# Fewer products in the FFN's down projection, set between the up products, on one core

## The chip, the cores and the metric

The kernel runs on one core of one Trainium2 chip. Its time is the device time of one execution in microseconds (us); of several runs the median counts. The engines of the core are named as in the profile: PE multiplies matrices, PEld is its weight load, DVE is the vector engine, ACT the scalar engine, POOL the GpSimd engine, SP the engine that issues most of the transfers. Each engine works off its own queue in the order in which the program wrote it.

## The reference, cut to what matters

The reference is one layer of a backbone over 1024 latent tokens of width 1024 with 256 context tokens: a state-space mixer (S5) with a gated linear unit, then a SwiGLU feed-forward network (FFN) with 2816 hidden units, and a last RMS norm. The change is in the FFN alone:

```python
h_l = modulate(rms_norm(x, norm_ffn[i]), m_l[3][:, None], m_l[4][:, None])
x = x + m_l[5][:, None] * swiglu(h_l, ffn_w1[i], ffn_w3[i], ffn_w2[i])
...
return rms_norm(x, norm_final)
```

Here `swiglu(h, w1, w3, w2)` is `(silu(h @ w1) * (h @ w3)) @ w2`. The two products with w1 and w3 are the up projection, the one with w2 the down projection. `m_l[5]` is a factor for each output column.

## The kernel before, in words

**Numbers.** All products are to float32 accuracy. An operand x is split into a high part, `hi`, which is x cast to the type fp32r, and a low part, `lo`, which is x minus `hi`. A product is then three matmuls: high by high, high by low, low by high. ACT makes the high part (a copy that casts, in `t_split` at line 1201, `split` at 1002, `gate_up` at 1270). The low part is a subtraction through the helper `tt`, so it stands at line 70 in the profile; for weights POOL does it (the argument `E`), for gated activations DVE.

**Tiling.** The 2816 hidden units are 22 tiles of 128, `ft` = 0 to 21. The 1024 tokens are held as 8 groups `s` of 128 and as two halves `n` of 512. `Y` holds the running sum x in SBUF and takes the results of the down projection. The up projection of tiles 0 and 1 is plain (`up_plain`). From tile 2 (`NPL`) on, `up` uses seven products instead of eight for the two token halves and the two halves of the inner dimension (a Strassen scheme in Winograd's form): product j of tile ft, called U0 to U6 below, is twelve matmuls, four blocks of 128 by three (`mm4`, `mm3`, lines 1259 to 1261), each 128x128 by 128x512. Its weight operand is a combination of four blocks `raw[:, 0..3]` of w1 and w3, which POOL forms in place (`prep`), and which is split into one of four slots of `ring`. A slot is free again when the product that used it is done.

**After an up product** DVE adds its PSUM bank to running sums in `t0` to `t3`, ACT applies SiLU, and `gate_up` multiplies and splits the gated result into the regions that the down projection reads as weights.

**Down projection.** After each `up(ft)`, `down([ft])` runs 16 chains of three matmuls, one for each token group s and each half of the output columns, over four PSUM buffers `pd`; DVE adds each chain to `Y` (128x512). The last `down([20, 21], True)` takes two tiles in one and also does the last norm. The w2 tile arrives in `w2raw` by a transfer on SP's queue (`raw2`); `load2` multiplies it on DVE with the column factor and splits it (1024 wide, POOL the low part).

**What sets the order.** The order of each queue is the order of the calls in the code, written out by hand (`manual_schedule`); the framework adds the waits. While `down([ft])` runs on PE, `prep(ft + 1)` steps between its chains prepare the next weights on POOL. The next tile's U0 is issued ahead of `down([ft])`. Transfers `raw13` fetch the blocks of w1 and w3 in three pieces as `raw` comes free.

Of the kernel before, what the change touches and what calls it, by code (L numbers as in the profile page):

```python
# [10 lines left out]
F32 = mybir.dt.float32  # L11
# [6 lines left out]
P = 128  # L18
# [19 lines left out]
def s5_ffn_kernel(tc, a, out):  # L38
# [3 lines left out]
    with ctx:  # L42
        ctx.enter_context(tc.manual_schedule())
        sb = ctx.enter_context(tc.tile_pool(name="sb", bufs=1))
        def region(tag, kb, dt=F32):
            return sb.tile([P, int(kb * 256)], dt, tag=tag, name=tag)

        def view(reg, kb, shape, parts=P):
            off = int(round(kb * 256))
            n = int(np.prod(shape))  # L50
            v = reg[:parts, off:off + n]
            if len(shape) > 1:
                names = "abcdef"[:len(shape)]
# [15 lines left out]
        def tt(o, x, y, op, eng=V):  # L69
            eng.tensor_tensor(out=o, in0=x, in1=y, op=op)  # L70
# [1175 lines left out]
        def gb(ft):  # L1246
            return GB[ft == NFT - 1]

        def raw2(ft):
            SY.dma_start(w2raw, a["w2"][ft * P:(ft + 1) * P])  # L1250

        def load2(ft):
            tt(w2raw, w2raw, MB[:, 1], MUL)
            split(w2raw, gb(ft)[2:], E)
            if ft + 1 < NFT:
                raw2(ft + 1)

# [102 lines left out]
        def prep(ft):  # L1360

            if ft > NPL:
                op_split(ft, 1, raw[:, 1])
                yield
# [11 lines left out]
        def mm(ft, j):  # L1376
            pu = pu_()
            mm4(pu, OP_[ft, j], BV[j], True, True)
            return pu

        def up(ft, pu, at={}):

            t0, t1, t2, t3 = tmp
            more = ft + 1 < NFT

            def go(j):
                if j in at:
                    at[j]()

            S.copy(t0, pu)  # L1390
            op_split(ft, 4, raw[:, 3])
            go(0)
            if more:
                raw13(ft + 1, 0, 1)
                raw13(ft + 1, 2, 4)
            tt(t1, mm(ft, 1), t0, ADD)
            S.activation(t1, t1, AF.Silu)
            op_split(ft, 5, raw[:, 1])
            if more:
                raw13(ft + 1, 1, 2)  # L1400
            go(1)
            tt(t0, mm(ft, 2), t0, ADD)
            op_split(ft, 6, s5)
            go(2)
            tt(t2, mm(ft, 3), t0, ADD)
            go(3)
            if more:
                op_split(ft + 1, 0, raw[:, 0])
            pu = mm(ft, 4)
            nx = prep(ft + 1) if ft == NFT - 2 else iter(())  # L1410
            next(nx, None)
            next(nx, None)
            tt(t3, t2, pu, SUB)
            tt(t1, t1, t3, MUL)
            gate_up(ft, 0, t1)
            tt(t0, mm(ft, 5), t0, ADD)
            next(nx, None)
            pu = mm(ft, 6)
            tt(t0, pu, t0, ADD)
            S.activation(t0, t0, AF.Silu)  # L1420
            tt(t2, pu, t2, ADD)
            pu = mm(ft + 1, 0) if more else None
            tt(t0, t0, t2, MUL)
            gate_up(ft, 1, t0)
            for _ in nx:
                pass
            return pu

        def down(fts, last, *others):
            for s in range(T):  # L1430
                for n in range(2):
                    pd = pf([512])
                    x2 = Y[:, 4 * n:4 * n + 4, s]
# [44 lines left out]
        h2s(7, tba[1], 1)  # L1478
        raw2(0)
        rest = iter(())  # L1480
        up_plain(0, 0, rest, {2: lambda: together(h2t_steps(7, pf, tba[1], 0), h2t_steps(7, pf, tba[1], 1)), 3: lambda: mod_row(1, pf)})
# [13 lines left out]
        pF = psF.__enter__()  # L1495
        NPU[0] = 4
        pu = mm(NPL, 0)
        down([NPL - 1], False, prep(NPL))

# [3 lines left out]

        for ft in range(NPL, NFT - 1):
            load2(ft)
            pu = up(ft, pu, {j: t1_go for j in range(4)} if ft == NPL else {})
            if ft < NFT - 2:
                down([ft], False, prep(ft + 1))
        up(NFT - 1, pu, {2: lambda: load2(NFT - 1)})
        SY.dma_start(NFb.rearrange("p k n -> p (k n)"), a["norm_final"].to_broadcast([P, D]))  # L1510
# [60 lines left out]
```

## Time and profile before

| | |
|---|---|
| timed runs | 1083.35, 1086.05, 1090.47 us; median 1086.05 us |
| profiled execution | span 1084.0 us from the first to the last instruction; no other time of it is listed |
| matmuls | 6088 |
| PE, DVE, POOL, ACT busy | 990.4, 762.3, 631.4, 418.7 us |
| the stretch with up products of seven | about 496 to 1054 us |

In the profile's groups a name such as `ru` or `c` is a memory region (buffer numbers left out), `pu` and `pd` are the PSUM banks of up and down products; `out<-in` names what is written and read, followed by partitions x elements and type. A count stands behind x. Times are us, means of one instruction ns. In the timeline a row gives start, duration, engine, line and operation; in square brackets the idle time before it and who ended it. A row of the windows view gives, for a stretch of the span, the busy time of each engine with its count of instructions, then the granted PE clock, the share of the transfer engines, and GB/s.

### The profile page before, as it was taken

How to read it: one execution, taken by the hardware profiler on the slowest of the kernel's cores; microseconds unless marked ns; L12 is line 12 of the kernel's file. 1: busy time of each engine (PE TensorE's matmuls, PEld its weight loads, DVE VectorE, ACT ScalarE, POOL GpSimd, SP SyncE). 2: the span in 40 equal slices, each digit the busy share in tenths (PEclk: the TensorE clock that was granted, in tenths of full speed). 3: DMA queues.
4: the chain of work that ended last, by engine and by line, in shares of the span. 5: the costliest groups of instructions: out<-in, count | busy, mean ns of one | idle time of the engine just before them, and what ended most of it. 6: DMA issues, size and time to landing. Idle time of an engine off the chain costs nothing.

```text
span 1084.0 us, 16631 instructions
## 1 busy us (share of the span) xinstructions
PE 990.4 (91%) x6088; PEld 790.4 (73%) x6088; DVE 762.3 (70%) x1783; ACT 418.7 (39%) x833; POOL 631.4 (58%) x501
## 2 busy tenths in 40 slices
PE   4898795656899999999999999999999999999997
PEld 1466521345799997887888888888888888888875
DVE  8979699970665686898766666666766666666657
ACT  4477620453964565423122222222222222222236
POOL 4599666881274364966565555665555555556563
PEclk9998997987999999999999999999999999999999
DMA  8966679675333102110111111111011111111104
GB/s 310 318 124 125 187 231 312 185 142 118 104 114 116 42 2 78 59 38 21 58 59 59 59 59 59 59 59 32 31 56 59 59 59 59 60 59 59 55 23 156
DMA packets 54946, 104.60 MB, mean 96 GB/s; under 512 B 4432, under 2 KB 25168, under 8 KB 53840
## 3 DMA queue, kind: packets, MB, share of 16 engines
q1 hardware_dynamic: 46656, 85.57, 23.7%
q0 software_dynamic: 3888, 14.16, 7.0%
q10 hardware_dynamic: 4320, 3.81, 1.1%
q8 instruction: 48, 0.79, 0.3%
q14 instruction: 34, 0.28, 0.1%
HBM read 83.20 MB, written 6.16 MB: 82 GB/s over the span
## 4 chain that ended last, share of the span: by engine, by line
PE 71%; DMA 9%; POOL 6%; DVE 6%; ACT 5%; issue 2%; SPq 1%; ACTq 0%; DVEq 0%; POOLq 0%
PE pu L1261 11%; PE pu L1260 11%; PE pu L1259 11%; PE pd L1259 7%; PE pd L1260 7%; PE pd L1261 7%; PE pe L1024 3%; PE pe L1025 3%; PE pe L1023 3%; DVE ru L70 2%; POOL c L70 2%; DMA c<-in_ada_w 2%; DMA kd<-r 1%; PE pm L514 1%; DVE rxa L70 1%
## 5 line engine op out<-in xcount | busy, mean ns | idle before, releaser
L70 POOL TENSOR_TENSOR c<-rxc,c 128x512 fp32r<-128x512 f32 x128 | 167.8, 1326 | 185.1 <-ACT c L1201 180.2
L70 DVE TENSOR_TENSOR ru<-pd,ru 128x512 f32<-128x512 f32 x336 | 226.5, 690 | 0.0
L1259 PE MATMUL pu<-ra,c 128*128 128x512 f32 x432 | 168.4, 390 | 0.6 <-ACT ra L1201 0.3
L1261 PE MATMUL pu<-ra,c 128*128 128x512 f32 x432 | 168.4, 390 | 0.6 <-POOL c L70 0.6
L1260 PE MATMUL pu<-ra,c 128*128 128x512 f32 x432 | 168.2, 389 | 0.6 <-DVE ra L70 0.6
L1201 ACT CAST c<-rxc 128x512 fp32r<-128x512 f32 x128 | 76.8, 617 | 188.0 <-POOL rxc L70 107.3
L1259 PE MATMUL pd<-c 128*128 128x512 f32 x336 | 131.0, 390 | 0.7 <-DVE ru L70 0.7
L1260 PE MATMUL pd<-c 128*128 128x512 f32 x336 | 130.7, 389 | 0.0
L1261 PE MATMUL pd<-c 128*128 128x512 f32 x336 | 130.7, 389 | 0.0
L70 DVE TENSOR_TENSOR ru<-pu,ru 128x512 f32<-128x512 f32 x84 | 57.8, 688 | 83.2 <-PE pu L1261 52.4
L70 POOL TENSOR_TENSOR c<-ru,c 128x1024 fp32r<-128x1024 f32 x22 | 53.0, 2407 | 81.7 <-ACT c L1002 73.0
L1261 PEld LDWEIGHTS pu<-ra,c 128*128 128x128 f32 x432 | 81.1, 188 | 18.5 <-POOL c L70 1.7
L1259 PEld LDWEIGHTS pu<-ra,c 128*128 128x128 f32 x432 | 81.1, 188 | 18.1 <-ACT ra L1201 0.8
L1260 PEld LDWEIGHTS pu<-ra,c 128*128 128x128 f32 x432 | 81.1, 188 | 17.7 <-POOL c L70 0.9
L1259 PE MATMUL pu<-c,c 128*128 128x512 f32 x192 | 74.9, 390 | 0.0
L1261 PE MATMUL pu<-c,c 128*128 128x512 f32 x192 | 74.7, 389 | 0.0
L1260 PE MATMUL pu<-c,c 128*128 128x512 f32 x192 | 74.7, 389 | 0.0
L1259 PEld LDWEIGHTS pd<-c 128*128 128x128 f32 x336 | 63.1, 188 | 15.0 <-DVE ru L70 1.9
L1261 PEld LDWEIGHTS pd<-c 128*128 128x128 f32 x336 | 63.1, 188 | 13.2
L1260 PEld LDWEIGHTS pd<-c 128*128 128x128 f32 x336 | 63.1, 188 | 12.9
L70 POOL TENSOR_TENSOR c<-rxc,rxa 128x1024 f32<-128x1024 f32 x30 | 62.0, 2138 | 16.2 <-PE pw L655 10.4
L70 DVE TENSOR_TENSOR ru<-ru,rxa 128x512 f32<-128x512 f32 (+1 forms) x62 | 62.5, 1008 | 7.1 <-ACT ru L1420 3.1
(333 smaller groups left out, 2137.3 us busy)
## 6 DMA issues: line engine op xcount, KB each, us to landing
c<-in_ada_w SPq DMA_DIRECT2D x64, 256.0 KB, 5.4
ru<-in_w SPq DMA_DIRECT2D x22, 512.0 KB, 3.6
c<-c POOLq DMA_DIRECT2D x20, 512.0 KB, 6.7
rxc<-in_w SPq DMA_DIRECT2D x38, 256.0 KB, 4.5
rxc<-in_w SPq DMA_DIRECT2D x19, 512.0 KB, 5.1
ra<-in_ada_w SPq DMA_DIRECT2D x10, 512.0 KB, 11.9
ru<-in_xT SPq DMA_DIRECT2D x4, 1024.0 KB, 8.5
ra<-kd SPq DMA_DIRECT2D x16, 256.0 KB
```

Source lines behind the costliest of these rows:

```text
L70: eng.tensor_tensor(out=o, in0=x, in1=y, op=op)
L514: PE.matmul(pm[32 * b:32 * b + 2], sc3[:, k, 1 - h:3 - h], ada_tile(i), start=i < 4, stop=i >= 60, tile_position=(0, 32 * b))
L1023: PE.matmul(pz, h_[:, k], wH[:, k], start=n == 0, stop=False)
L1024: PE.matmul(pz, h_[:, k], wL[:, k], start=False, stop=False)
L1025: PE.matmul(pz, l_[:, k], wH[:, k], start=False, stop=n == 7)
L1201: S.copy(o[0], x)
L1259: PE.matmul(pu, wh, bh, start=start, stop=False)
L1260: PE.matmul(pu, wh, bl, start=False, stop=False)
L1261: PE.matmul(pu, wl, bh, start=False, stop=stop)
```

## The change

Tiles 2 to 19 are now taken in nine pairs (f, f+1), f = 2, 4, ..., 18 (`PAIRS`). The down projection of a pair is a product of two by two blocks (token halves by hidden tiles, hidden tiles by column halves), and it too is done by seven products, D1 to D7, with twelve matmuls each: four token groups by three. Tiles 20 and 21 keep the plain `down`, as does tile 1.

- **Order.** One list `seq` fixes the order on PE. For each f after the first: U0 U1 D6 D2 D5 D3 U2 D4 U3 U4 U5 U6 of tile f, where the D are those of the pair before, then for tile f+1 U0 D1 U1 U2 D7 U3 U4 U5 U6, where the D are of the pair itself. (The text marks products of tile f+1 with a dash: U0' to U6'.)
- **Weights' ring.** D products take their w2 operand from the same four-slot ring: `produce(i + 4)`, called after product i, makes the operand of product i+4. For D1 and D6, D4 it also forms block combinations of w2 on POOL, 512 wide.
- **w2.** There are two raw tiles (`w2r`, the second in a new region `RW` of 6 KB); DVE multiplies each with the column factor (`gate2`, after U3 and U4 of tile f).
- **Gated activations.** `post_u` writes the four blocks to `rA`, `rB`, `rC`, `t3` and combines them with DVE (`after_u` too); ACT makes the high parts and DVE the low parts in `GS`, at places spread over `post_u`, `after_u` and `post_d`.
- **PSUM.** D1, D7, D6, D5, D4 run in two tiles of two banks (`XT`), D2 and D3 in the four banks `UT` that the U products rotate through. D7, D6, D5 and D3 add onto what stands in the banks. After each D, `d_adds` adds the banks to quarters of `Y`: two adds of 128x1024 from `XT`, or four of 128x512 from `UT`.
- **Y.** `to_diff` and `from_diff` turn parts of `Y` to differences and back once (four adds of 1024 each on DVE, after U5 of tile 2 and after U3 and U5 of tile 20).
- The reserve for descriptors of POOL's transfers is set to 8192 bytes.

```diff
+        RW = region("rw", 6)
...
-        w2raw = view(RU, 32, [D])
+        w2r = [view(RU, 32, [D]), view(RW, 0, [D])]
...
+        def gate2(ft):
+            tt(w2r[ft % 2], w2r[ft % 2], MB[:, 1], MUL)
...
-        def up(ft, pu, at={}):
...
+        XT = [pF.tile([P, 2, 512], F32, tag=f"x{i}", name=f"xt{i}") for i in range(2)]
+        UT = [pF.tile([P, 512], F32, tag=f"u{i}", name=f"ut{i}") for i in range(4)]
...
+        rA, rB, rC = R0[:, 0:512], R0[:, 1036:1548], view(RW, 4, [512])
...
+        PAIRS = range(NPL, NFT - 2, 2)
+        seq = []
+        for f in list(PAIRS) + [NFT - 2]:
+            U = [("U", f, j) for j in range(7)]
+            if f == NPL:
+                seq += U
+            else:
+                M = {j: ("D", f - 2, j) for j in range(2, 7)}
+                seq += [U[0], U[1], M[6], M[2], M[5], M[3], U[2], M[4]] + U[3:]
+            if f in PAIRS:
+                U = [("U", f + 1, j) for j in range(7)]
+                seq += [U[0], ("D", f, 1), U[1], U[2], ("D", f, 7)] + U[3:]
+        seq += [("U", NFT - 1, j) for j in range(7)]
...
+        def cut(o, x):
+
+            t_split(o, x, V)
+
+        def produce(i):
...
+            if kind == "D":
+                x = w2_op(j)
+                (b11, b12), (b21, b22) = WB
+                if j == 6:
+                    tt(b12, b22, b11, SUB, E)
+                elif j == 4:
+                    tt(b21, b21, b12, SUB, E)
+                t_split(o, x, E)
+                if j == 1:
+                    tt(b11, b12, b11, SUB, E)
+                    tt(b12, b22, b12, SUB, E)
+                if j == 4:
+                    raw2(ft + 2)
+                    raw2(ft + 3)
+                return
+            x = (raw[:, 0], raw[:, 1], raw[:, 0], raw[:, 2], raw[:, 3], raw[:, 1], s5)[j]
+            t_split(o, x, E)
+            if j == 0:
+                tt(s5, raw[:, 2], raw[:, 3], ADD, E)
+            elif j == 1:
+                tt(raw[:, 2], raw[:, 0], raw[:, 2], SUB, E)
+                tt(raw[:, 0], s5, raw[:, 0], SUB, E)
+            elif j == 3:
+                tt(raw[:, 1], raw[:, 1], raw[:, 0], SUB, E)
+                if ft + 1 < NFT:
+                    raw13(ft + 1, 0, 1)
...
+        def d_mm(i):
...
+            for s, pd in d_banks(i, j):
+                cs_ = slice(s * P, s * P + P)
+                for n, (w, b) in enumerate(((gh, wh), (gh, wl), (gl, wh))):
+                    PE.matmul(pd, w[:, cs_], b, start=j in (1, 2, 4) and n == 0, stop=n == 2,
+                              skip_group_check=j not in (1, 2, 4))
+
+        def d_adds(i, j):
...
+            if j in (2, 3):
+                for s, pd in d_banks(i, j):
+                    y = Y[:, k0:k0 + 4, s0 + s]
+                    tt(y, y, pd.rearrange("p (k n) -> p k n", k=4), op)
+            else:
+                for h in range(2):
+                    y = quad(k0, s0, h)
+                    tt(y, y, XT[h].rearrange("p s (k n) -> p s k n", k=4), op)
...
+        def post_u(i, ft, j):
+
+            pu, plain, f = u_bank(i), ft >= NFT - 2, ft % 2 == 0
+            if j == 0:
+                S.copy(t0, pu)
+            elif j == 1:
+                tt(t1, pu, t0, ADD)
+                S.activation(t1, t1, AF.Silu)
...
+            elif j == 4:
+                tt(t3, t2, pu, SUB)
...
+                    r = rA if f else rC
+                    tt(r, t1, t3, MUL)
+                    cut(GS[0], r)
...
+            else:
+                tt(t0, pu, t0, ADD)
+                S.activation(t0, t0, AF.Silu)
+                tt(t2, pu, t2, ADD)
...
+                elif f:
+                    tt(rB, t0, t2, MUL)
+                    tt(rA, rA, rB, SUB)
+                else:
+                    tt(t3, t0, t2, MUL)
+                    tt(rA, t3, rA, SUB)
+
+        def after_u(ft, j):
...
+            if j == 0:
+                hi(GS[1], rA)
+                tt(rC, rA, rC, SUB)
+                lo(GS[1], rA)
+                hi(GS[2], rC)
+            elif j == 1:
+                tt(rB, rB, t3, ADD)
+                hi(GS[3], rB)
+                lo(GS[2], rC)
+
+        def post_d(i, j):
+
+            if j == 1:
+                hi(GS[1], rA)
+            d_adds(i, j)
+            if j == 1:
+                lo(GS[1], rA)
+            elif j == 6:
+                lo(GS[3], rB)
+            elif j == 2:
+                hi(GS[0], t3)
+                lo(GS[0], t3)
...
+        for i, (kind, ft, j) in enumerate(seq):
+            if i:
+                (u_mm if kind == "U" else d_mm)(i)
+            if kind == "D":
+                post_d(i, j)
+            else:
+                post_u(i, ft, j)
+                after_u(ft, j)
+                if ft in PAIRS and j in (3, 4):
+                    gate2(ft + j - 3)
+            produce(i + 4)
+            if kind == "U":
+                if ft == NPL and j < 4:
+                    t1_go()
+                if ft == NPL and j == 5:
+                    to_diff()
...
+    nc = bacc.Bacc("TRN2", target_bir_lowering=False, num_devices=1, dynamic_dma_scratch_size=8192)
```

The functions `hi` and `lo` are one ACT copy that casts and one DVE subtraction.

More of the change, by code (lines that the diff above doesn't have):

```diff
@@ L1373, in prep, with pd_ @@
             tt(raw[:, 1], raw[:, 1], raw[:, 0], SUB, E)
+            raw13(ft + 1, 0, 1)
             yield
[L1376 to L1379, printed above, removed]
-        def up(ft, pu, at={}):
[L1383 to L1427, printed above, removed]
+        def pd_(i):
+            return ([XT[0][:, 0], XT[1][:, 0]] + UT[1:])[i % 5] if XT is not None else pf([512])
+        XT = None
         def down(fts, last, *others):
@@ new lines, in quad, with to_diff, from_diff, hi @@
+        def quad(k0, s0, h):
+            return Y[:, k0:k0 + 4, s0 + 2 * h:s0 + 2 * h + 2].rearrange("p k s n -> p s k n")
+        def to_diff():
+            for h in range(2):
+                tt(quad(4, 0, h), quad(4, 0, h), quad(4, 4, h), SUB)
+                tt(quad(4, 0, h), quad(4, 0, h), quad(0, 0, h), SUB)
+        def from_diff(h):
+            tt(quad(4, 0, h), quad(4, 0, h), quad(4, 4, h), ADD)
+            tt(quad(4, 0, h), quad(4, 0, h), quad(0, 0, h), ADD)
+        def hi(o, x):
+            S.copy(o[0], x)
@@ new lines, in after_u @@
+        def after_u(ft, j):
+            if not (ft > NPL and ft <= NFT - 2 and ft % 2 == 0):
+                return
+            if j == 0:
[15 more added lines that the diff above has]
+                lo(GS[3], rB)
+            elif j == 2:
+                hi(GS[0], t3)
+                lo(GS[0], t3)
@@ L1502, in t1_go @@
                 next(rest, None)
[L1504 to L1509, printed above, removed]
+        u_mm(0)
+        down([NPL - 1], False, prep(NPL))
+        raw2(NPL)
+        raw2(NPL + 1)
+        for i, (kind, ft, j) in enumerate(seq):
[3 more added lines that the diff above has]
+                post_d(i, j)
+            else:
+                post_u(i, ft, j)
[8 more added lines that the diff above has]
+                    to_diff()
+                if ft == NFT - 2 and j in (3, 5):
+                    from_diff(j // 4)
+                if ft == NFT - 2 and j == 4:
+                    load2(NFT - 2)
+                if ft == NFT - 1 and j == 2:
+                    load2(NFT - 1)
         SY.dma_start(NFb.rearrange("p k n -> p (k n)"), a["norm_final"].to_broadcast([P, D]))
```

62 lines of the change are left out of this document (49 added, 13 removed).

## The prediction

> **What bounds the kernel now.** I read the page's first and fourth parts, then the windows inside the FFN, then what PE waited for.
>
> ```profile
> span 1084.0 us, 16631 instructions
> ...
> PE 990.4 (91%) x6088; PEld 790.4 (73%) x6088; DVE 762.3 (70%) x1783; ACT 418.7 (39%) x833; POOL 631.4 (58%) x501
> ...
> PE 71%; DMA 9%; POOL 6%; DVE 6%; ACT 5%; issue 2%; SPq 1%; ACTq 0%; DVEq 0%; POOLq 0%
> ```
> ```profile
> 830.00:880.00 50.00, 50.00 (x223) 41.39 (x222) 32.99 (x47) 13.39 (x22) 30.21 (x23) 1.00 0.19 63
> 880.00:930.00 50.00, 50.00 (x222) 41.42 (x221) 36.85 (x53) 11.44 (x19) 26.40 (x20) 1.00 0.10 33
> ```
> ```profile
> PE pd L1259 <- DVE ru L70: 0.7, 2, 0.4
> ```
> ```profile
> 658.99 0.39 PE L1259 MATMUL pu<-c,c 128*128 128x512 f32 x1
> ...
> 688.91 0.39 PE L1259 MATMUL pu<-c,c 128*128 128x512 f32 x1
> ```
>
> In the windows PE is busy for all of 50 us at granted clock 1.00; in the whole run its down products waited 0.7 us for DVE. So here PE's count of matmuls is the time. The last two rows are the first matmul of U0 in two neighbouring tiles: 29.92 us for 84 + 48 = 132 matmuls, 0.2267 us each (not the 0.39 of a row, which overlaps the next). A product of twelve takes 2.72 us.
>
> **What is removed.** Two tiles cost 2 x 48 = 96 down matmuls; seven products cost 84. Nine pairs save 9 x 12 = 108 matmuls, 108 x 0.2267 = 24.5 us, all on the path. A pair would take 252 x 0.2267 = 57.1 us instead of 59.8. The gain is lost if PE comes to wait 24.5 / 9 = 2.7 us a pair. So everything hangs on who feeds PE.
>
> **Loads of the feeders.** Durations:
>
> ```profile
> L70 DVE TENSOR_TENSOR ru<-pd,ru 128x512 f32<-128x512 f32 x239 | 162.7, 691 | 0.0
> L70 POOL TENSOR_TENSOR c<-rxc,c 128x512 fp32r<-128x512 f32 x90 | 115.8, 1301 | 149.0 <-ACT c L1201 145.6 <-PE pu L1261 3.4
> ...
> L1201 ACT CAST c<-rxc 128x512 fp32r<-128x512 f32 x89 | 53.5, 617 | 146.7 <-POOL rxc L70 81.2 <-DMA rxc<-in_w 60.8 <-PE pu L1260 4.8
> ...
> L70 POOL TENSOR_TENSOR rxc<-rxc 128x512 f32<-128x512 f32 x30 | 39.0, 1300 | 1.2
> L70 POOL TENSOR_TENSOR c<-ru,c 128x1024 fp32r<-128x1024 f32 x15 | 36.2, 2410 | 51.9 <-ACT c L1002 51.9
> ...
> L70 DVE TENSOR_TENSOR c<-ru,c 128x512 fp32r<-128x512 f32 x28 | 19.7, 704 | 19.2 <-ACT c L1270 19.2
> ...
> L70 DVE TENSOR_TENSOR ru<-ru,rxa 128x1024 f32<-128x1024 f32 x15 | 18.2, 1216 | 0.0
> ```
>
> POOL had, for two tiles, 14 low parts, 8 combinations (1.30 each) and 2 low parts of w2 (2.41): 33.4 of 59.8 us. Now 21 low parts and 12 combinations: 33 x 1.30 = 42.9 of 57.1. DVE had 46 adds from PSUM (0.69), 8 ops on two SBUF inputs (0.70) and two w2 multiplications (1.22): 39.8. Now 22 adds of 512, 10 of 1024 from two banks, 15 ops on two SBUF inputs, the same two multiplications. No row shows the wide PSUM add: between 1.22 (the SBUF op of that width) and 1.38 (two narrow ones); I take 1.22, since the element count sets it. Sum 40.3. ACT rises to about 21 us. Nobody is full. What they share is:
>
> ```profile
> 670.29 1.29 POOL L70 TENSOR_TENSOR c<-rxc,c 128x512 fp32r<-128x512 f32 x1 [1.90 <-ACT c L1201]
> ```
> ```profile
> 670.86 1.27 DVE L70 TENSOR_TENSOR ru<-ru,rxa 128x512 f32<-128x512 f32 x1
> ```
> ```profile
> 462.36 1.46 POOL L70 TENSOR_TENSOR c<-rxc,c 128x512 fp32r<-128x512 f32 x1 [0.96 <-ACT c L1201]
> 463.77 1.75 POOL L70 TENSOR_TENSOR ra<-rxa,ra 128x512 fp32r<-128x512 f32 x1
> ```
> ```profile
> 462.59 1.78 DVE L70 TENSOR_TENSOR rxa<-ra,c 128x512 f32<-128x512 f32 x1
> ```
>
> A DVE op on two SBUF inputs that starts inside a POOL op ends 0.55 after it: 671.58 to 672.13, and 463.82 to 464.37. POOL's next op starts at 463.77 and lasts 1.75 instead of 1.30: it in turn waits. They take turns, whole instructions long. Adds from PSUM are not held (0.691 mean over 239 beside a busy POOL). By these rows the two exclude each other for 33 x 1.25 + 15 x 0.55 + 2 x 1.08 = 51.7 of 57.1 us. Before it was about 32 + 8 x 0.55 + 2.2 = 39 of 59.8. That is the crowding that the change brings.
>
> **The chain in order.** A matmul waits for its own operand alone (first row: one matmul, for DVE's low part). The others give the gaps between steps:
>
> ```profile
> 492.92 0.47 PE L1260 MATMUL pu<-ra,c 128*128 128x512 f32 x1 [0.64 <-DVE ra L70]
> ```
> ```profile
> 664.43 0.39 PE L1259 MATMUL pu<-ra,c 128*128 128x512 f32 x1
> ```
> ```profile
> 664.63 0.69 DVE L70 TENSOR_TENSOR ru<-pu,ru 128x512 f32<-128x512 f32 x1 [1.27 <-PE pu L1261]
> ```
> ```profile
> 645.59 0.69 DVE L70 TENSOR_TENSOR ru<-pu,ru 128x512 f32<-128x512 f32 x1 [1.61 <-PE pu L1261]
> 646.20 0.68 DVE L70 TENSOR_TENSOR rxa<-pu,rxa 128x512 f32<-128x512 f32 x1
> 646.98 0.69 DVE L70 TENSOR_TENSOR ru<-ru,rxa 128x512 f32<-128x512 f32 x1
> ```
> ```profile
> 646.31 0.63 ACT L1420 ACTIVATE ru<-ru 128x512 f32<-128x512 f32 x1 [3.66 <-DVE ru L70]
> ...
> 663.93 0.60 ACT L1201 CAST c<-rxc 128x512 fp32r<-128x512 f32 x1
> 664.46 0.62 ACT L1201 CAST c<-r 128x512 fp32r<-128x512 f32 x1
> ```
> ```profile
> 680.11 1.29 POOL L70 TENSOR_TENSOR r<-rxc 128x512 f32<-128x512 f32 x1
> 681.48 1.30 POOL L70 TENSOR_TENSOR rxc<-rxc 128x512 f32<-128x512 f32 x1
> ```
> ```profile
> 478.04 1.22 DVE L70 TENSOR_TENSOR ru<-ru,rxa 128x1024 f32<-128x1024 f32 x1
> 479.18 0.69 DVE L70 TENSOR_TENSOR rxa<-rxa,ra 128x512 f32<-128x512 f32 x1
> ```
>
> DVE sees a product 0.20 after its end (the next product's first matmul is at 664.43). DVE ops follow 0.61 apart, or after their input with 0.1 between; a wide one occupies 1.14. ACT ops follow 0.53 apart; POOL ops 1.25, or 1.37 on their own output.
>
> Now zero is the end of U4' of a pair. PE's plan without waits: U5' to 2.72, U6' to 5.44, U0 to 8.16, U1 to 10.88, then D6, D2, D5, D3, and U2 at 21.76.
> - DVE: t3 0.20, rC 0.99 to 1.67. ACT: high part of rC, then (queued behind it) of U1's weight, to 2.87. POOL: U1's low part from 2.94, its two combinations, then D6's combination: four ops, to 8.12.
> - Only then can ACT cast D6's weight (8.16 to 8.78), and the SiLU of U6' is queued behind this cast: 8.70 to 9.33, though U6' was over at 5.44.
> - DVE's product t3 wants to start at 9.37, inside POOL's low part for D6 (8.85 to 10.1): it ends at 10.65. POOL's low part for D2 then holds until 11.85, so rA = t3 - rA ends at 12.4. ACT's high part of it: 13.06. D6, planned for 10.88, starts at 13.1, and its third matmul waits 0.4 for the low part (13.9): **2.65 late**.
> - From 12.5 on DVE works through rC, low, add of U1, rB, low, two wide adds of D6, low, four adds of D2, low, two wide adds of D5, the first add of D3: 12.2 us by the spacings, and about 2 us held by POOL's low parts for D5, U2 and D4. It ends at 26.5. U2 writes the bank that this last add frees, so it starts at 26.55 instead of 21.76: **4.8 us a pair**, the 2.65 in it. Without the held ops the same chain gives 1.3 us; with wide adds at 1.38 and every op held, 5.8.
> - Second half: U4 ends, then t3, rA, its low part and the second w2 multiplication; that one frees POOL to form D1's second combination, then U1's low part and two combinations, the last of which U2' reads. With four DVE ops taking turns in between, U2's cast is done 0.4 late and its low part 0.9 more: **1.3 us**; nothing if no op is held, 2.0 if all are.
>
> Items that I cost at nothing: D1, D7 and D4 (their adds have three products of cover); ACT's extra casts; the w2 transfers, moved to SP's queue behind D4's low part, which have over 12 us to the multiplication that reads them. SP's three `raw13` pieces go out later than now; if U0's piece is late by its 4.5 us, the same chain starts about 0.6 later:
>
> ```profile
> rxc<-in_w SPq DMA_DIRECT2D x38, 256.0 KB, 4.5
> ```
>
> The smaller descriptor reserve touches POOL's transfers alone, which are over before 260 us; in the next rows they are issued 5.2 us apart. I take nothing; if each had to wait out its predecessor's 6.7 us to landing, about 1.5 us each for the 12 from 157 us on, most off the path: 0 to 10 us.
>
> ```profile
> 216.27 0.87 POOL L658 DMA_DIRECT2D c<-c  x1 [0.30 <-POOL c L70]
> 221.49 0.88 POOL L658 DMA_DIRECT2D c<-c  x1 [0.30 <-DMA c<-c]
> ```
> ```profile
> c<-c POOLq DMA_DIRECT2D x20, 512.0 KB, 6.7
> ```
>
> In tile 2 the four 1024-wide ops of `to_diff` fall on DVE at once, each taking turns with a POOL op: 4 x 2.3 = 9 us in front of the chain that feeds D7, which has four products (10.9 us) of cover less 3 us of its own chain and what POOL loses for U2'. Between 0 and 9; I take 4, once.
>
> **Sum.** D6 to U2 occurs nine times (tiles 4 to 20), the second half eight times beside tile 2: 1084.0 - 24.5 + 9 x 4.8 + 8 x 1.3 + 4 = 1117 us of span. The page lists no time beside the span; the median shown lies 2 above it, so 1119.
>
> **The clock** could make it worse:
>
> ```profile
> 240.00:248.00 8.00, 0.12 (x1) 0.16 (x1) 0.00 (x0) 2.15 (x6) 5.31 (x5) 0.50 0.60 122
> 248.00:256.00 8.00, 6.12 (x52) 5.25 (x52) 0.00 (x0) 0.00 (x0) 0.65 (x1) 0.76 0.73 142
> ...
> 488.00:496.00 8.00, 6.88 (x29) 4.83 (x28) 6.45 (x8) 2.01 (x4) 5.82 (x4) 1.00 0.18 63
> ```
>
> Idle for nearly 8 us, PE falls to 0.50; with 1.1 us idle in 8 it keeps 1.00. Pauses of 1.6 to 2.6 us lie between. I take no loss. If each of the 18 pauses cost what the second row lost (0.24 of 8 us, 1.9 us), it is 34 us more. The Trainium skill, "TensorE: Matmul & The Clock Gate", section "A second HAM failure mode: psum-queue depth-cycling", says that short pauses between groups of matmuls can already make the clock swing; the row at 488 speaks against it.
>
> **Rivals.**
> 1. *The held ops miss each other* (ends faster). Place: DVE's two-input ops from t3 to the last low part before D3. If POOL stands idle at these moments, only the 1.3 us chain is left: 1084 - 24.5 + 9 x 1.3 = 1071, or 1073 as a median. It decides at 2.7 us a pair. For it: in 646.98 the same multiplication met no POOL op. Against it: D6's cast starts both POOL's low part and, one SiLU later, DVE's multiplication, so these two meet every time. 0.14.
> 2. *Full gain*, as if all operands came in time: 1061.5. Against it: the chain from U4' to D6 alone is 11.5 us by rows for 10.88. 0.07.
> 3. *Transfers late on top*: 0.6 to 1 us more a pair and a worse tile 2: 1119 + 9 = 1128. 0.13.
> 4. *The clock swings*: 1119 + 34 = 1153. 0.05.
>
> That the change doesn't remove the matmuls is no rival: the count follows from the lists.
>
> **How the numbers follow.** The forecast keeps 0.61; its own range, by 3.3 to 5.8 us and 0 to 2 us in the two halves of a pair and 0 to 9 once, is 1091 to 1139. The range 1072 to 1136 leaves out rival 2, rival 4, half of rival 1 and the tip of the forecast: under 0.2. A measurement of this kernel tells a change of about 1% (11 us) from none: faster by more takes rivals 1 and 2 less a little, 0.18; within 1% the rest of rival 1 and the forecast's low end, 0.12; slower 0.70.
>
> **What would show it.** Right: 5980 matmuls; a pair takes about 63 us; PE waits about 2 us for ACT at D6's first matmul and about 1.6 us for DVE at U2's, in each pair; DVE's t3 multiplication lasts about 1.3 and the rA subtraction about 1.65; POOL's low part for D2 1.7. Wrong: PE is busy without gaps, DVE's two-input ops stay at 0.7, or PE's waits are for POOL or transfers. It would go most wrong where POOL is ahead of D6's combination, so that the SiLU isn't held.

## The result, and the profile after

The changed kernel takes 1123.29 us (median of 4 runs, 1120.65 to 1133.08), the kernel before on the same chip 1085.14: 1.038 times as long, 95% interval 1.032 to 1.044. It is slower by 38 us, where 33 were forecast. The first two lists are from the page of the changed kernel and from the list of what PE waited for (total us, times, longest); `ut` and `xt` are the PSUM tiles UT and XT.

```profile
span 1119.9 us, 16648 instructions
...
PE 992.8 (89%) x5980; PEld 776.4 (69%) x5980; DVE 839.2 (75%) x1728; ACT 455.4 (41%) x905; POOL 765.2 (68%) x582
...
PE 46%; DVE 18%; POOL 17%; DMA 7%; ACT 6%; issue 4%; SPq 1%; ACTq 0%; POOLq 0%; DVEq 0%
...
L71 DVE TENSOR_TENSOR ru<-ru,xt 128x1024 f32<-128x1024 f32 x90 | 107.5, 1213 | 15.1 <-PE xt L1541 12.3
```
```profile
PE xt L1541 <- ACT c L1571: 18.4, 9, 2.3
...
PE ut L1263 <- POOL c L71: 11.8, 11, 3.6
...
PE ut L1261 <- DVE ru L71: 11.2, 9, 1.4
```

The 108 matmuls are gone (6088 to 5980). But in the chain that ended last PE's share falls from 71% to 46%, and DVE and POOL, with 6% each before, hold 35%. PE's nine waits for ACT are those of D6, the nine for DVE those of U2, in nine groups of interleaved products.

One such group, from the timelines of DVE, ACT, POOL and PE. The product U4' ended at 831.25, 0.20 ahead of the first row:

```profile
831.45 0.69 DVE L71 TENSOR_TENSOR rxa<-rxa,ut 128x512 f32<-128x512 f32 x1 [2.03 <-PE ut L1263]
...
840.56 1.36 DVE L71 TENSOR_TENSOR rxa<-ru,rxa 128x512 f32<-128x512 f32 x1 [2.38 <-ACT ru L1601]
841.95 1.65 DVE L71 TENSOR_TENSOR r<-rxa,r 128x512 f32<-128x512 f32 x1
```
```profile
833.50 0.62 ACT L1202 CAST c<-rxc 128x512 fp32r<-128x512 f32 x1
839.37 0.62 ACT L1202 CAST c<-ru 128x512 fp32r<-128x512 f32 x1 [5.26 <-POOL ru L71]
839.90 0.63 ACT L1601 ACTIVATE ru<-ru 128x512 f32<-128x512 f32 x1
```
```profile
838.06 1.28 POOL L71 TENSOR_TENSOR ru<-rw,ru 128x512 f32<-128x512 f32 x1
840.07 1.30 POOL L71 TENSOR_TENSOR c<-ru,c 128x512 fp32r<-128x512 f32 x1 [0.73 <-ACT c L1202]
841.32 1.72 POOL L71 TENSOR_TENSOR c<-rw,c 128x512 fp32r<-128x512 f32 x1
```
```profile
844.30 3.29 PE L1541 MATMUL xt<-c,c 128*128 128x512 f32 x12 [2.01 <-ACT c L1571]
847.43 2.88 PE L1541 MATMUL ut<-c,c 128*128 128x512 f32 x12
850.15 3.31 PE L1541 MATMUL xt<-c,c 128*128 128x512 f32 x12
853.31 2.88 PE L1541 MATMUL ut<-c,c 128*128 128x512 f32 x12
857.57 0.47 PE L1261 MATMUL ut<-ra,c 128*128 128x512 f32 x1 [1.38 <-DVE ru L71]
```

The reader sees the chain link by link. POOL finishes D6's combination at 839.3; ACT has stood 5.26 us for it, and the SiLU of U6' goes only behind that cast. DVE's t3 product starts inside POOL's low part for D6 and ends 0.55 behind it (841.37 to 841.92); POOL's low part for D2 lasts 1.72 because it waits in turn; the rA subtraction lasts 1.65. D6 starts at 844.30, and U2, which waits for DVE, at 857.57.

**Where the time is in the run.** The transfers of the first 430 us vary between executions: the first down product of tile 0 came at 422.3 here and at 429.1 in the profile of before. Comparisons between profiles are therefore made from the first down product to the end of the span (its start is in the first row of the tile's list):

```profile
L1259 PE MATMUL pd<-c x336: 389/389/504, 429.1 to 1074.6; 128*128 128x512 f32 x168
```
```profile
L1261 PE MATMUL pd<-c x16: 389/389/497, 422.3 to 433.7; 128*128 128x512 f32 x16
```

Before: 1084.0 - 429.1 = 654.9 us; after: 1119.9 - 422.3 = 697.6, that is 42.7 more. (The table ahead of the prediction puts the start of the stretch with seven products at about 496 us; it begins earlier: U1 of tile 2 starts at 477 in the profile before.) The parts, each against its matmuls at 0.2267 us:

- From U1 of tile 2 (470.37) to the first D6 (526.97): 17 products, 46.2 us, took 56.6; without D6's own wait of 2.2 us, 8.2 lost.
- From D6 to D6, eight times (526.97 to 1035.28): 63.5 us a pair instead of 57.1, 6.4 lost each.
- From the last D6 (1035.28) to the last `down` (1090.19): 17 products took 54.9; without the 2.4 us up to U2, 6.3 lost.

### The profile page after: what moved, and what is told of

Same layout as the page of the kernel before. It is cut to its first block, busy times and chain, and to the rows that moved or that the text cites. A ratio compares the mean times of both kernels' runs of the same rounds, so it can differ in the third digit from the quotient of the medians.

```text
span 1119.9 us, 16648 instructions
## 1 busy us (share of the span) xinstructions
PE 992.8 (89%) x5980; PEld 776.4 (69%) x5980; DVE 839.2 (75%) x1728; ACT 455.4 (41%) x905; POOL 765.2 (68%) x582
## 4 chain that ended last, share of the span: by engine, by line
PE 46%; DVE 18%; POOL 17%; DMA 7%; ACT 6%; issue 4%; SPq 1%; ACTq 0%; POOLq 0%; DVEq 0%
PE ut L1263 7%; DVE ru L71 7%; PE ut L1261 7%; PE ut L1262 7%; PE xt L1541 7%; POOL c L71 6%; POOL rxc L71 6%; DVE c L71 3%; POOL ru L71 3%; PE pe L1025 3%; PE pe L1026 3%; PE pe L1024 3%; DVE r L71 2%; DVE rxa L71 2%; DMA c<-in_ada_w 1%
## 5 line engine op out<-in xcount | busy, mean ns | idle before, releaser
L1261 PE MATMUL ut<-ra,c 128*128 128x512 f32 x400 | 158.7, 397 | 13.1 <-DVE ru L71 11.2
L1263 PE MATMUL ut<-ra,c 128*128 128x512 f32 x400 | 158.3, 396 | 9.2 <-POOL c L71 9.2
L1541 PE MATMUL xt<-c,c 128*128 128x512 f32 x540 | 142.2, 411 | 18.9 <-ACT c L1571 18.4
L1262 PE MATMUL ut<-ra,c 128*128 128x512 f32 x400 | 156.7, 392 | 0.0
L1541 PEld LDWEIGHTS xt<-c,c 128*128 128x128 f32 x540 | 104.7, 197 | 49.8 <-ACT c L1571 22.2
L71 DVE TENSOR_TENSOR ru<-ru,xt 128x1024 f32<-128x1024 f32 x90 | 107.5, 1213 | 15.1 <-PE xt L1541 12.3
L1261 PEld LDWEIGHTS ut<-ra,c 128*128 128x128 f32 x400 | 75.9, 190 | 35.1 <-ACT c L1202 20.4
L71 POOL TENSOR_TENSOR c<-ru,c 128x512 fp32r<-128x512 f32 (+1 forms) x39 | 59.0, 1514 | 59.8 <-ACT c L1202 45.5
L1263 PEld LDWEIGHTS ut<-ra,c 128*128 128x128 f32 x400 | 75.9, 190 | 29.3 <-POOL c L71 13.6
L71 DVE TENSOR_TENSOR ru<-ut,ru 128x512 f32<-128x512 f32 x98 | 67.2, 686 | 37.7 <-PE ut L1263 36.0
L1262 PEld LDWEIGHTS ut<-ra,c 128*128 128x128 f32 x400 | 75.7, 189 | 15.4
L1263 PE MATMUL ut<-c,c 128*128 128x512 f32 x160 | 62.9, 393 | 2.6 <-POOL c L71 2.6
L1261 PE MATMUL ut<-c,c 128*128 128x512 f32 x160 | 62.7, 392 | 0.0
L1262 PE MATMUL ut<-c,c 128*128 128x512 f32 x160 | 62.7, 392 | 0.0
L71 POOL TENSOR_TENSOR rxc<-rxc 128x512 f32<-128x512 f32 x40 | 57.9, 1448 | 0.1
L1541 PE MATMUL ut<-c,c 128*128 128x512 f32 x216 | 52.2, 391 | 0.0
L569 PE MATMUL pv<-ru,c 128*64 128x160 f32 x512 | 45.3, 315 | 3.9 <-ACT ru L488 2.0
## 6 DMA issues: line engine op xcount, KB each, us to landing
ra<-in_ada_w SPq DMA_DIRECT2D x10, 512.0 KB, 11.9
```

The costliest lines, as they stand in the source:

```text
L569: PE.matmul(pv[64 * (i % 2):64 * (i % 2) + 64, ri, c0:c0 + 160], w[:, i, 64 * ri:64 * ri + 64], U[:, 8 * b + 4 * j + i], start=True, stop= ...
L1261: PE.matmul(pu, wh, bh, start=start, stop=False)
L1262: PE.matmul(pu, wh, bl, start=False, stop=False)
L1263: PE.matmul(pu, wl, bh, start=False, stop=stop)
L1541: PE.matmul(pd, w[:, cs_], b, start=j in (1, 2, 4) and n == 0, stop=n == 2, skip_group_check=j not in (1, 2, 4))
```

## The experiments

The chain has three suspects in it: ACT's queue (the SiLU behind D6's cast), the mutual exclusion of DVE and POOL, and the clock. Beside them stand the differences formed in `Y` at both ends. The experiments were timed in three later groups, in which the kernel before took 1082.88, 1080.66 and 1081.76 us; each ratio below is to the kernel before in its own group.

### D6's combination earlier

```diff
-                if j == 6:
-                    tt(b12, b22, b11, SUB, E)
...
+                if j == 7:
+                    tt(b12, b22, b11, SUB, E)
```

> D6's combination of w2 blocks is formed on POOL right behind D7's low part, 14 products earlier, instead of behind U1's three ops. Nothing else moves. Theory A (the forecast: ACT's cast for D6 waits for POOL, and the SiLU of U6' waits behind that cast): DVE's t3 multiplication starts about 2 us earlier, PE's wait for ACT at D6 falls from 2.0 us to under 0.5, the whole DVE chain to U2 comes 2 us earlier, and nine pairs give 18 us: about 1105 us. Rival B (DVE's own queue from the add of U1 on is the bound, the cast only changes where PE waits): the wait at D6 goes, the wait at U2 grows by as much, about 1123 us as now.

1103.89 us (1100.39 to 1104.79), 1.018 of before (1.015 to 1.021); 676.1 us from the first down product. A move of one POOL op gives 19 us; 18 were expected. (In `seq` the move is seven products, from ahead of the operand for D6 to behind the one for D7, and not the 14 that the expectation names; by POOL's rows it is 16 us.) The wait for ACT at D6 is gone; at its third matmul D6 now waits for DVE's low part in most pairs, as the rows show, and U2 waits as long as it did. PE rows of one pair:

```profile
770.18 2.56 PE L1541 MATMUL xt<-c,c 128*128 128x512 f32 x10 [0.29 <-DVE c L71]
782.72 0.47 PE L1261 MATMUL ut<-ra,c 128*128 128x512 f32 x1 [1.39 <-DVE ru L71]
```

So the SiLU behind the cast set the start of DVE's chain, and the chain from there on is a bound of its own. Rival B, by which U2 would wait the longer, falls.

### Second inputs from PSUM

```diff
-                    tt(t3, t0, t2, MUL)
-                    tt(rA, t3, rA, SUB)
+                    tt(t3, t0, pu, MUL)
+                    tt(rA, pu, rA, SUB)
...
-                tt(rC, rA, rC, SUB)
-                lo(GS[1], rA)
+                tt(rC, pu, rC, SUB)
+                tt(GS[1][1], rA, pu, SUB)
...
-                tt(rB, rB, t3, ADD)
+                tt(rB, rB, pu, ADD)
...
-                lo(GS[2], rC)
+                tt(GS[2][1], rC, pu, SUB)
```

> In the six DVE ops t3 = t0*t2, rA = t3 - rA (after U6'), rC = rA - rC and the low part of GS[1] (after U0), rB = rB + t3 and the low part of GS[2] (after U1), one of the two SBUF inputs is replaced by the PSUM bank of the U product just done. The result is not the reference's; counts, sizes and queues stay, and the low parts no longer need the high part. Theory A (DVE and POOL hold each other up over two-input SBUF ops): these six last 0.69 each, rA comes 1.5 us earlier, the chain to U2 about 2.6 us earlier, nine pairs 24 us: about 1099 us; PE's wait at D6 about 0.6 instead of 2.0. Rival B (their long rows in the profile are waits for something else, or the chain is set by ACT's held SiLU alone): t3 and rA keep 1.3 and 1.65, about 1120 us.

1101.98 us (1100.75 to 1103.37), 675.5 from the first down product; 1099 were expected. PE's wait at D6 fell to 0.26:

```profile
772.72 3.30 PE L1541 MATMUL xt<-c,c 128*128 128x512 f32 x12 [0.26 <-ACT c L1571]
785.67 0.47 PE L1261 MATMUL ut<-ra,c 128*128 128x512 f32 x1 [1.40 <-DVE ru L71]
```

With the order of all queues unchanged, six ops that read one SBUF input instead of two give 21 us. (The low parts among them also wait for no high part; the experiment with products in place, below, shows the row lengths without that.) The exclusion costs about as much as ACT's queue, and the two overlap: each edit alone takes most of D6's wait away.

### Matmuls in the pause

PE's pause at D6 was filled with eight matmuls into a bank that D2 overwrites.

```diff
+            if j == 6:
+                for k in range(8):
+                    PE.matmul(u_bank(i), RG[(i - 1) % 4][0][:, k % 4], BV[1][0][:, :, k % 4], start=True, stop=True)
```

> Eight additional matmuls (1.8 us) are set in front of each D6, where PE now waits 2 us; they write a PSUM bank that D2 then overwrites, so the result stays. Theory A (the clock drops after some of the pauses at D6, but U2's start is set by DVE's chain, so PE's slow matmuls are made up by a shorter wait at U2): the granted clock stays 1.00 at D6, PE's wait at U2 rises to 1.4 in all pairs, and the time falls by 0 to 5 us, 1118 to 1123. Rival B (the clock is a cost of its own): 1.6 us in each pair with a clock below 1, and more in its neighbours: 8 to 15 us less, 1108 to 1115. If PE's pause were not idle time but hidden work, it would rise by 9 x 1.8 = 16 us, to 1139.

1170.69 us: a miss, and not for any of these reasons. The slot that the filler read belonged, at that place of the program, to D3's weights already, so PE waited for their cast, 46 us in nine times:

```profile
PE ut L1539 <- ACT c L1202: 46.0, 9, 5.1
```

The second filler reads D6's own weights, `RG[i % 4]`.

> The filler before D6 again, but its eight matmuls read D6's own weight operand, which is ready 4 us before D6 starts; the first filler read a ring slot that already belonged to a later product and so waited 5.1 us for a cast. Theory A (U2's start is set by DVE's chain; the slow clock at D6 in about half the pairs is made up at U2): clock 1.00 at D6, its twelve matmuls 2.9 to 3.3 us in every pair, the wait at U2 1.4 in every pair, time 0 to 5 us lower, 1118 to 1123. Rival B (the clock costs of its own): 1108 to 1115.

1123.69 us (1122.63 to 1125.29): no change in the time, and 694.8 against 697.6 from the first down product. Windows of the changed kernel at five of its nine D6 (the granted clock stands third from the end; the other four show 0.66 once and 1.00 three times), then the PE rows of one D6 with the filler, and a window of it:

```profile
590.00:595.00 5.00, 5.00 (x15) 3.67 (x16) 4.91 (x6) 3.09 (x6) 3.33 (x2) 0.66 0.00 0
653.00:658.00 5.00, 4.30 (x12) 3.15 (x13) 4.97 (x6) 3.50 (x6) 2.92 (x2) 0.72 0.00 0
...
780.00:785.00 5.00, 4.62 (x12) 3.38 (x13) 5.00 (x6) 3.21 (x6) 3.24 (x2) 0.66 0.01 2
844.00:849.00 5.00, 4.70 (x19) 3.60 (x20) 5.00 (x7) 3.75 (x7) 3.33 (x3) 1.00 0.00 0
907.00:912.00 5.00, 4.76 (x13) 3.52 (x14) 4.93 (x6) 3.07 (x6) 3.33 (x2) 0.66 0.00 0
```
```profile
783.68 1.98 PE L1539 MATMUL ut<-c,c 128*128 128x512 f32 x8
785.88 3.29 PE L1544 MATMUL xt<-c,c 128*128 128x512 f32 x12 [0.22 <-ACT c L1574]
```
```profile
780.00:800.00 20.00, 18.28 (x77) 13.85 (x77) 17.82 (x20) 8.87 (x15) 15.49 (x11) 1.00 0.19 59
```

After a pause of 2 us the clock fell to about 0.66 for the next product in five of nine pairs, and D6 took up to 4.9 us instead of 3.3. With the filler it stays at 1.00 at all nine. But U2 waits for DVE's adds, so the slow product is for the most part made up: from D6 to U2 it is 14.2 us in a slow pair (780.38 to 794.61) and 13.3 in a fast one (844.30 to 857.57), 1 us. Five such pairs would be 5 us. From the first to the last D6 the filler did give 4.7 (503.6 us against 508.3), over the whole stretch 3, and nothing that the medians can show. The clock is a consequence of the waits here, and not their cause.

### Without the differences in Y

```diff
-                    to_diff()
+                    pass
...
-                    from_diff(j // 4)
+                    pass
```

> The eight 1024-wide DVE ops of to_diff (after U5 of tile 2) and from_diff (after U3 and U5 of tile 20) are left out, so the output is not the reference's. Theory A (they and POOL's ops take turns and hold U1' and U2' of both stretches): PE's waits between U6 of tile 2 and D7 (about 7 us with the slow clock behind them) and the 3.6 us wait at U2' of tile 21 go: 8 to 11 us less, 1112 to 1115. Rival B (the first and last tiles are late for other reasons, the steps of T and load2): under 3 us, 1120 or more.

1114.08 us (1110.4 to 1117.31), 687.4 from the first down product: 9 to 10 us less, as expected. In the changed kernel the four ops of `to_diff` took 8.35 us of DVE in one row, and POOL's ops beside them 2.2 instead of 1.3:

```profile
490.29 8.35 DVE L71 TENSOR_TENSOR ru<-ru 128x1024 f32<-128x1024 f32 x4
```
```profile
493.09 2.24 POOL L71 TENSOR_TENSOR c<-rxc,c 128x512 fp32r<-128x512 f32 x1
495.30 2.26 POOL L71 TENSOR_TENSOR rxc<-rxc 128x512 f32<-128x512 f32 x1
497.63 2.15 POOL L71 TENSOR_TENSOR rxc<-r,rxc 128x512 f32<-128x512 f32 x1
```

`from_diff` had been left out of the sum. With `load2` it made the wait of 3.59 us for POOL at U2 of tile 21, which is gone here (the longest wait of that kind is 1.3):

```profile
1075.49 0.80 PE L1263 MATMUL ut<-ra,c 128*128 128x512 f32 x1 [3.59 <-POOL c L71]
1075.50:1078.50 3.00, 3.00 (x7) 2.44 (x8) 1.18 (x2) 1.83 (x4) 2.94 (x3) 0.50 0.00 0
```

The last row is a window behind that wait: the clock is at 0.50, and the next matmuls come 0.43 us apart.

The two ends share the gain: from U1 of tile 2 to the first D6, 3.9 us are lost beside D6's own wait instead of 8.2, and after the last U2 0.8 instead of 6.3. So nearly all of the loss at the end is `from_diff` with what it delays, but about half of the loss in tiles 2 and 3 is there without `to_diff`: U1' waits 1.3 us for POOL, U2' 1.2 for ACT and 0.6 for POOL. What makes these operands late was not looked into further.

### Low parts on POOL

This is the first experiment, with the low parts for D3, D5 and D4 moved from DVE to POOL (`lo(..., E)` at the three places in `after_u` and `post_d`).

> As e1, and the three low parts for D3 (GS[2]), D5 (GS[3]) and D4 (GS[0], second filling) are made by POOL instead of DVE. Theory A (the rest of the loss of e1, 4.0 us a pair, is DVE's chain from U1 to U2 with its held ops): DVE's chain is shorter by three ops and their waits, about 3.3 us, U2 no longer waits, a pair takes 58 to 58.5 us instead of 61.1: nine pairs give about 24 us over e1's 1104, 1080. Rival B (POOL, three ops fuller, becomes late for D5, D4 and U2, and the exclusion costs the same from the other side): 1100 to 1110, with PE's waits for POOL.

1090.63 us (1086.47 to 1096.74), 1.009 of before (1.005 to 1.013); 664.2 from the first down product, 11.9 less than the first experiment. This lies between the two theories (1080, and 1100 to 1110). U2 no longer waits; a pair takes 59.8 us, not 58 to 58.5. What stays are three waits in a pair: D6 and D5 at their third matmul, U2' for POOL.

```profile
768.52 2.58 PE L1541 MATMUL xt<-c,c 128*128 128x512 f32 x10 [0.29 <-DVE c L71]
770.94 2.88 PE L1541 MATMUL ut<-c,c 128*128 128x512 f32 x12
773.66 0.61 PE L1541 MATMUL xt<-c,c 128*128 128x512 f32 x2
774.64 2.60 PE L1541 MATMUL xt<-c,c 128*128 128x512 f32 x10 [0.36 <-POOL c L71]
805.74 0.50 PE L1263 MATMUL ut<-ra,c 128*128 128x512 f32 x1 [0.62 <-POOL c L71]
```

D5's third matmul would have come at 773.66 + 2 x 0.227 = 774.11; it came 0.53 later, with 0.36 in the row. A wait costs more than its row says, because the row counts from the modelled end of the matmul before. Three waits a pair at that rate, with 0.15 to 0.3 us that the matmuls beside each wait are late as well (ten from 768.52 take 2.42 us, not 2.27), are the 2.7 us.

### The ends spread, and w2's combinations later

The eight ops of `to_diff` and `from_diff` are set one or two behind a product, `load2` of both last tiles goes into tile 21, and the combinations behind D1 go behind U2':

```diff
+            elif j == 2:
+                if ft - 1 in PAIRS:
+                    (b11, b12), (b21, b22) = WB
+                    tt(b11, b12, b11, SUB, E)
+                    tt(b12, b22, b12, SUB, E)
...
+                if ft == NPL and j in (5, 6):
+                    diff(j - 5, SUB)
+                if ft == NPL + 1 and j == 0:
+                    diff(2, SUB)
+                    diff(3, SUB)
+                if ft == NFT - 1 and 2 <= j < 6:
+                    diff(j - 2, ADD)
+                if ft == NFT - 1 and j in (2, 4):
+                    load2(NFT - 3 + j // 2)
```

> As e5, and further: the eight ops of to_diff and from_diff are set one or two behind a product instead of in blocks, w2 of tiles 20 and 21 is prepared within tile 21, and the two combinations behind D1 are formed behind U2' instead, so that U1' and U2' come sooner. Theory A (each wait of PE that is named so far goes: 9 x 0.62 at U2', 5 of the 7 us of tile 2, 4 of the 6 us of tiles 20 and 21): 14 us under e5, about 1065, and so about 18 us under the kernel before. Rival B (the moved ops hold up others: D7's cast waits for its combination and holds ACT, the spread ops lengthen DVE's chain): no better than e5.

1092.05 us (1088.38 to 1094.15), 661.9 from the first down product: no better in the medians than the experiment before, so theory A failed and rival B held. U2' no longer waits, and a pair takes 59.2 us. But three of the spread ops met again in DVE's queue, one behind the other, ahead of D1's adds, and D7 of tile 2 waited 4.2 us for them:

```profile
500.73 6.72 DVE L71 TENSOR_TENSOR ru<-ru 128x1024 f32<-128x1024 f32 x3
507.37 2.34 DVE L71 TENSOR_TENSOR ru<-ru,xt 128x1024 f32<-128x1024 f32 x2
```

### The descriptor reserve alone

The kernel before, with `dynamic_dma_scratch_size=8192`.

> The kernel before with nothing but the descriptor reserve of 8192 bytes. In the profiles so far the first down product comes at 422 to 425 us with the change and at 429 without. Theory A (the reserve costs or gives nothing; the 7 us are the spread of the transfers of the first 430 us between executions): time equal to the kernel before within 0.5%, and the first down product anywhere between 420 and 430. Rival B (it sets the start): 5 to 7 us less than before, the first down product at 422.

1081.65 us beside 1080.66 for the kernel before, ratio 1.001 (0.9985 to 1.0034), and the first down product at 427.4. The reserve gives and costs nothing, and the earlier start in the profile of the changed kernel doesn't come from it. Across all profiles the start lies between 422.3 and 429.1. The programs of the two experiments that follow are alike up to this product, and on one chip it came at 422.9 in the first and at 428.5 in the second; so executions spread by that much without a change in the program. That the transfers make this spread is likely, but was not shown.

### Gated products in place in PSUM

```diff
+                    tt(pu, t2, pu, SUB)
+                    tt(pu, t1, pu, MUL)
+                    cut(GS[0], pu)
+                    S.copy(rA if f else rC, pu)
...
+                    tt(pu, pu, t2, ADD)
+                    tt(pu, t0, pu, MUL)
+                    if f:
+                        tt(rA, rA, pu, SUB)
+                    else:
+                        tt(rA, pu, rA, SUB)
+                    S.copy(rB if f else t3, pu)
```

> In the changed kernel the gated products of U4 and U6 are formed in place in the PSUM bank of the product (t2 and pu, then t1 or t0 and pu), the subtraction for rA reads that bank, and ACT copies the block to SBUF afterwards. Result and order stay; six two-input SBUF ops of DVE a pair become ops with one PSUM input, ACT has four copies more. Theory A (DVE and POOL exclude each other over two-input SBUF ops): the t3 product and the rA subtraction last 0.7 each, PE's wait at D6 falls from 2.0 to about 0.5, the chain to U2 comes 1.7 us earlier, 15 us in nine pairs, about 1108. Rival B (the long rows were waits for inputs): they stay long, and the copies make ACT later: 1123 or more.

1133.68 us (1132.47 to 1136.56), 10 us slower than the changed kernel, where 15 less were expected. The rows say that the half of theory A on the exclusion holds and that the gain was lost on ACT and, behind it, to the clock (DVE rows first, then ACT, then D6 and a window at D6; U4' ended at 771.11):

```profile
781.75 0.69 DVE L71 TENSOR_TENSOR ut<-ru,ut 128x512 f32<-128x512 f32 x1 [3.70 <-ACT ru L1602]
782.47 0.69 DVE L71 TENSOR_TENSOR r<-ut,r 128x512 f32<-128x512 f32 x1
```
```profile
774.18 0.59 ACT L1597 COPY rw<-ut 128x512 f32<-128x512 f32 x1 [0.76 <-DVE c L71]
774.66 0.62 ACT L1202 CAST c<-rxc 128x512 fp32r<-128x512 f32 x1
```
```profile
785.36 5.52 PE L1541 MATMUL xt<-c,c 128*128 128x512 f32 x12 [3.21 <-ACT c L1571]
785.30:790.30 5.00, 4.94 (x12) 3.69 (x13) 4.64 (x5) 2.82 (x6) 2.42 (x3) 0.50 0.00 2
```

The t3 product and the rA subtraction last 0.69 beside a busy POOL, instead of 1.36 and 1.65. But the copy of the block waits 0.76 for DVE's low part from the same bank, and U1's cast, which heads POOL's four ops, comes 3.55 us after U4' instead of 2.25 (833.50 - 831.25). Everything behind it is 1.3 us later, and the second copy stands in front of the cast that D6 waits for: D6 waits 3.2 us. After this longer pause the granted clock is at 0.50 to 0.70 at all nine D6, whose twelve matmuls take 4.9 to 5.5 us, and DVE's second wide add waits 0.94 us for them; how much of the loss is the clock and how much ACT was not separated. By these rows, in this kernel ACT's queue, not DVE, is the thing to keep short between U4' and D6 until D6's combination is out of the way.

### All of it

The kernel with the ends spread, with the products in place, the low part for D5 ahead of that for D3, and only those two ops of `to_diff` ahead of D1 that must be there (the two that subtract the first quarter).

> All of it: e6 with the gated products in place as in e10, the low part for D5 ahead of the one for D3 on POOL, and of to_diff only the two ops that must be ahead of D1 left there, the other two after U3 and U4 of tile 3. Theory A: no wait at D6 over 0.2, none at D5, none of 4.2 at D7 of tile 2; a pair 57.3 to 57.8 us instead of 59.2 in e6, nine pairs 13 to 17 us, 4 more in tile 2: about 1073, under the kernel before (1081). Rival B (a next bound stands right behind: POOL and DVE with 52 of 57 us of mutual exclusion, or ACT with 60 ops): 1082 to 1092, with new waits at other products.

1072.19 us (1069.49 to 1075.39), 0.991 of the kernel before (0.989 to 0.993), 645.0 from the first down product against 654.9. With D6's cast free of POOL's four ops, the in-place products and the new order of the low parts do give a gain: a pair takes 57.8 us instead of 59.2. What each of the two gave was not separated; D5's wait for POOL is gone too. From tile 4 on all that is left of PE's waits is 0.2 us at D6's third matmul (first row). The longest that remain are at the end, where the weights of tile 21 for the last `down` are late:

```profile
816.78 2.57 PE L1543 MATMUL xt<-c,c 128*128 128x512 f32 x10 [0.21 <-DVE c L71]
1039.99 0.80 PE L1261 MATMUL xt<-ra 128*128 128x512 f32 x1 [3.06 <-ACT ra L1003]
1042.86 0.79 PE L1262 MATMUL xt<-ra 128*128 128x512 f32 x1 [2.07 <-POOL ra L71]
```

So the 24.5 us of removed matmuls are real; 10 of them are a gain once the queues are put in another order. The kernels with the ends spread call the `load2` of tile 21 two products later than the changed kernel, which has no such waits; an earlier call in the new order was not tried.

## Why the prediction was right, point by point

- **The removed work**: 108 matmuls at an unchanged 0.2267 us, as forecast.
- **The chain to D6**: right to 0.1 us. Forecast from U4': t3 product 9.37 to 10.65, rA ready 12.4, D6 at 13.1; measured 9.31 to 10.67, 12.35, 13.05. The first experiment (the cast) and the second (the exclusion) each took most of the wait away, so both links are shown and not only argued.
- **The chain from rA to U2**: forecast 26.55, measured 26.32 (857.57 - 831.25); U2's wait went when three ops left DVE. The wide PSUM add, taken at 1.22, measured 1.213.
- **The second half of a pair**: 1.3 forecast. A pair without the slow clock (844.30 to 907.24) took 62.9 us, 5.8 above its matmuls; up to U2 it lost 4.6, which leaves about 1.2.
- **Tile 2**: the term was mis-sized. 4 us stood in the sum, 0 to 9 in the bounds; 8.2 were lost. The 9 us of DVE were right (8.35 measured). What had too little weight is POOL: four of its ops beside them were stretched to 2.2 each, and U1' and U2' read what the last of them make. Without `to_diff` 3.9 of the 8.2 are still lost, against 1.2 in the second half of other pairs, and this part the sum didn't have at all.
- **Tiles 20 and 21**: the step that failed. The sum charged nothing after the last U2; 6.3 us were lost there. `from_diff` is the same four ops as `to_diff`, and it met `load2`'s wide op on POOL; without it 0.8 us were lost.
- **The clock**: "I take no loss" was wrong in what it says of the clock. Pauses of 2 us were enough in five of nine pairs. By a row with 1.1 us of idle time the prediction set aside what the Trainium skill says in "TensorE: Matmul & The Clock Gate", section "A second HAM failure mode: psum-queue depth-cycling": that short pauses between groups of matmuls can already make the clock swing. These rows agree with it (0.66 after 2.0 us). The price of the slow clock was small in a pair, 1 us in a slow one, because U2 waits for DVE anyway. At the two ends PE has no such wait to make it up: behind the last wait there (0.63 us at U2' of tile 3, soon after one of 1.22, and 3.59 us at U2 of tile 21) the clock was at 0.50, about 1.5 us lost each.
- **What made the total come out**: over the stretch after the first down product the forecast was 33 us more and the profile shows 42.7. The profile of the changed kernel began that stretch 6.8 us earlier than that of before, and by medians the difference is 38. The sum is right in its main term: for the nine stretches from D6 to U2 and the eight second halves 53.6 us were forecast and 55.8 lost, some 5 of them to the slow clock. It is short by 4 and 6 us at the two ends. That 1117 us of span stand so near to the measured 1119.9 is in part luck: the earlier start hid 6.8 us.
- **The rivals**: that the held ops miss each other was refused by the rows, as its counter-argument said: the same two ops meet in every pair. Late transfers did not show: no wait of PE or ACT in a pair is for one.

## What to carry to other kernels

A cast that waits for a slow engine holds whatever is queued behind it: look at what stands behind the op that waits before asking what the op itself costs. When matmuls are removed from a stretch in which PE was full, count again the ops that feed each product, above all those that exclude each other (two-input SBUF ops of DVE against POOL), by their place in time and not by their sum. The best single remedy here that kept the result moved one op of the slow engine seven products earlier. Shorter ops gave as much where they cost nothing (21 us, but not with the reference's result); made correct by two more ACT copies in each tile they cost 10 us, and they paid only in a kernel in which D6's cast had been freed.

## What the runs showed of the hardware

- A DVE op on two SBUF inputs waits for POOL's op in progress and ends 0.55 us behind it, in every group shown; with one input from PSUM it lasts 0.69 beside the same POOL ops. On which ops contend, the Trainium skill says the same in "SBUF — State Buffer", section "Who interferes with whom": a DVE instruction with at most one SBUF input, outside certain fast modes, doesn't contend with GpSimd. The trace agrees (1.36 and 1.65 against 0.69).
- What had not been expected: the granted clock fell to 0.66 after a pause of 2 us in five of nine cases that are alike, and stayed at 1.00 in the other four. After pauses of 3.2 us, in the run with the products in place, it fell in all nine (0.50 to 0.70).
- A copy on ACT that reads a PSUM bank stood until DVE's read of that bank was over (0.76 us; the second copy of the pair 1.48 us), although both only read. Whether the chip or the program's waits demand it was not tried.
